# Overlapped mixing units, seeds copied into PSUM, and weight forms kept apart by size, in a hybrid RG-LRU, retention and gated-convolution block

## The chip, the cores and the metric

The kernel runs on one core of a Trainium2 chip. The time is the device time of one execution in microseconds (us), taken as the median over runs. TensorE is called PE (its weight loads PEld), VectorE DVE, ScalarE ACT, and SyncE, which issues the loads of the weights, SP.

## What is computed

One layer over 512 tokens and 16 meta tokens (528 positions), width 1024, in float32:

```python
xn = rms_norm(h, norm_mix_g[l])
z = xn @ w_in[l]
u_rnn, u_gate, q, k, v, g_ret, ga, gb = jnp.split(z, IN_SPLITS, axis=-1)
xr = causal_dwconv(u_rnn, rnn_conv_w[l], rnn_conv_b[l])
hr = rg_lru(xr, rg_a_w[l], rg_a_b[l], rg_x_w[l], rg_x_b[l], lru_lambda[l])
o_a = hr * jax.nn.gelu(u_gate)
...
o = retention(q, k, v.reshape(bsz, t, RET_HEADS, RET_DV))
o_b = head_rms(o).reshape(bsz, t, RET_HEADS * RET_DV) * jax.nn.silu(g_ret)
mixed = (jax.nn.sigmoid(ga) * (o_a @ w_branch_rnn[l])
         + jax.nn.sigmoid(gb) * (o_b @ w_branch_ret[l]))
h = h + mixed @ w_out[l]
xn = rms_norm(h, norm_ffn_g[l])
up = causal_dwconv(xn @ w_up[l], ffn_conv_w[l], ffn_conv_b[l])
gate, val = jnp.split(up, 2, axis=-1)
h = h + (jax.nn.gelu(gate) * val) @ w_down[l]
```

The end is one more RMS norm, over the 512 tokens. The change touches the values `v`, the gates `g_ret`, `ga` and `gb`, and the two branches that `mixed` sums up.

## The kernel before

**Split matmuls.** Each float32 operand is split into two float16 parts, high and low (`split`, lines 94 to 97: ACT writes the high part, L95, DVE the low one, L96), and a product takes three matmuls, high by high, high by low and low by high.

**Units of weights.** The weights are cut into units of up to 1 MB. A unit is loaded into one of three buffers `raw` (`wraw`, on SP's queue, L107), and preparation steps split it into tiles `wt` of 4 KB a partition (`wsp`, ten of them). The load of a unit takes the buffer of the unit three before it, so it waits until the last form of that one has been cut by DVE. `tick` runs preparation steps ahead of their use as long as the units from the current one on need no more than `ahead[0]` tiles; a fast unit counts four, another two.

**Fast units.** A fast unit replaces the eight block products of a 2 x 2 block multiplication by seven, with sums of weight blocks (`fast_steps`: B11, B21 with B22, three sums on DVE at L263 to L265, then T1 with T3 and T4 with T2) and sums of input blocks prepared earlier (F3, F5, F6, F7). `fast_products` (product at L929) runs them in this order, which the calls of `advance` name P1, P7, P6, P2, P5, P3, P4: B11 into a PSUM bank `pa`, T3 into `pe`, T2 onto `pa`, B21 into `pb`, T1 onto `pa`, B22 onto `pa`, T4 onto `pe`. Between them ACT copies what stands in `pa` to SBUF (`keep`, L935, tiles `kept` and `last`), and DVE adds these copies to `pb` (L954) and `pe` (L959, L967). A product has 12 matmuls in a gate unit and 24 in a unit of the second branch. At the end a function is applied: a sigmoid or another gate on ACT (L976), or a multiplication by the gate on DVE (L1244). PSUM has four banks for this from the values of head 1 on (`psum_layout(acc=2, bank=4)`), beside two `acc` tiles of two banks each.

**The stages around the change.** Values of heads 1, 2 and 3 (`fast_values`, product at L1027), each followed by the retention output and its gate (`retention_out`, `gated`), up to about 425 us; then the mix stage to 638 us. There `gate_a` runs a unit of `ga` and the first branch (`branch`, ten blocks of w_branch_rnn, tile `pm`, matmuls at L435), whose result is multiplied by the gate in `mix_first` (DVE, `m`, L1265); `head_norm(3)` sums the squares of the last head (matmul L1110, square root on ACT L1112); and `gate_b` runs a unit of `gb` and then `mix_products`, two units of w_branch_ret at once, whose result is added to `m` (L1250) and split into `mx`. The units of the two branches are mixed in the order that the lists `u_ga`, `u_ba`, `u_gb` and `u_bb` are filled in. After 638 us come the output projection, the up projection (to about 934 us) and the down projection.

**Order on an engine.** Each engine takes its instructions in the order of the program, moved by a scheduler: what stands under `tc.high_priority()` goes ahead of other ready work, and `issue_after(last_keep[0])` holds an instruction behind the last copy out of a bank (`behind_copy`, used for the late steps of a fast unit while `gating` holds). A waiting instruction holds up everything behind it on its engine.

Of the kernel before, what the change touches and what calls it, by code (L numbers as in the profile page):

```python
# [15 lines left out]
P = 128  # L16
# [38 lines left out]
def hybrid_block_kernel(ctx, tc, x, meta, norm_mix_g, w_in, conv_w, conv_b, rg_a_w, rg_a_b,  # L55
# [4 lines left out]
    xp = ctx.enter_context(tc.tile_pool(name="xp", bufs=4))  # L60
    pieces = ctx.enter_context(tc.tile_pool(name="pieces", bufs=46))
    wraw = ctx.enter_context(tc.tile_pool(name="wraw", bufs=3))
    wsp = ctx.enter_context(tc.tile_pool(name="wsp", bufs=10))
    work = ctx.enter_context(tc.tile_pool(name="work", bufs=8))
    small = ctx.enter_context(tc.tile_pool(name="small", bufs=4))
    psum = {}
# [13 lines left out]
    def bank(name):  # L80
        return psum["bank"].tile([P, 512], F32, name=name, tag="bank")
# [9 lines left out]
    def wtile(name):  # L91
        return work.tile([P, T], F32, name=name, tag="w")
# [59 lines left out]
    def add_ba():  # L152
        u_ba.append(unit(10, P, [(0, 0, kmaj(w_brnn, 0, 10, P * len(u_ba), P))]))

    def add_gate(us, o):
        us.append(unit(8, 256, [(0, 0, kmaj(w_in, 0, 8, o + 256 * len(us), 256))], fast=True))

    def add_bb():
        i = len(u_bb) // 2
        for g in range(2):  # L160
            rows = w_bret[8 * P * g:8 * P * (g + 1)].rearrange("(i j p) c -> p j i c", i=4, j=2)
            u_bb.append(unit(8, 256, [(4 * j, 0, rows[:, j, :, 256 * i:256 * i + 256]) for j in range(2)], fast=True))

    for i in range(2):
# [1 line left out]
        add_ba()  # L166
        add_gate(u_gr[3], o_gr + 1536)
        add_ba()
    add_gate(u_ga, o_ga)
    add_ba()  # L170
    add_ba()
    for i in range(4):
        add_gate(u_gb, o_gb)
        add_bb()
        if i == 0:
            add_gate(u_ga, o_ga)
        if i < 2:
            add_ba()
    u_out = [unit(2, 1024, [(0, 0, kmaj(w_out, 2 * a, 2, 0, 1024))]) for a in range(4)]
    u_up = []  # L180
    for j in range(12):
# [62 lines left out]
    def fast_steps(rv, bk, bc):  # L244


        tiles = []
        top, low = slice(0, bk), slice(bk, 2 * bk)
        left, right = slice(0, bc), slice(bc, 2 * bc)

        def cut(rows, cols):
            def run():
                t = wsp.tile([P, 2, 1024], F16, name="wt")
                src = rv[:, rows, cols]
                n = bk * src.shape[2]
                tv = [t[:, a, :n].rearrange("p (k c) -> p k c", k=bk) for a in range(2)]
                tiles.append(tv)
                split(tv[0], tv[1], src, SW)
            return run

        def sums():
            pair = rv[:, top].rearrange("p k (h c) -> p h k c", h=2)
            nc.vector.tensor_tensor(pair, pair, rv[:, :, right].rearrange("p (h k) c -> p h k c", h=2), op=ALU.add)  # L263
            nc.vector.tensor_tensor(rv[:, low, right], rv[:, top, left], rv[:, low, right], op=ALU.add)
            nc.vector.tensor_tensor(rv[:, low, left], rv[:, low, left], rv[:, low, right], op=ALU.add)  # L265

        at = {"B11": (0, 0), "B21": (1, 0), "B22": (1, bc), "T1": (2, 0), "T3": (2, bc), "T4": (3, 0), "T2": (3, bc)}

        def form(nm, a, k):
            i, c0 = at[nm]  # L270
            return tiles[i][a][:, k, c0:c0 + bc]

        def late(run):
            def behind():
                with behind_copy():
                    run()
            behind.late = True
            return behind

        wviews.append(form)  # L280
        return [cut(top, left), cut(low, slice(0, 2 * bc)), sums,
                late(cut(top, slice(0, 2 * bc))), late(cut(low, slice(0, 2 * bc)))]
# [11 lines left out]
    current = [0]  # L294

    def unit_tiles(u):
        return 4 if units[u][3] else 2

    def emit_step():
        u, run = steps[done[0]]  # L300
        while len(loaded) < min(u + 3, len(units)):
            queue(unit_load())
        run()
        done[0] += 1

    def queue(new):
# [552 lines left out]
    def rest(run):  # L859
        for _ in run:  # L860
            pass
# [58 lines left out]
    def fast_products(ws, src, func, finish, n=257):  # L920


        last_k = 4 * len(ws) - 1
        c1 = n - 257

        def product(ps, wf, xf_, first=False):
            for k in range(last_k + 1):
                for aw, ax in SPLIT:
                    nc.tensor.matmul(ps[:, :n], ws[k // 4](wf, aw, k % 4), src(xf_, ax, k),  # L929
                                     start=first and k == 0 and (aw, ax) == (0, 0), stop=k == last_k and aw == 1,  # L930
                                     skip_group_check=True)

        def keep(dst, ps, c0):
            with tc.high_priority():
                last_keep[0] = nc.scalar.activation(dst, ps[:, c0:c0 + 257], AF.Copy).ins  # L935

        kept, last = wtile("kept"), wtile("last")
        g0, g1 = wtile("g0"), wtile("g1")
        h0, h1 = slice(0, 257), slice(257, TQ)
        pa = bank("pa")  # L940
        product(pa, "B11", "A11", True)
        keep(kept[:, h0], pa, 0)
        close_tails()
        yield
        pe = bank("pe")
        product(pe, "T3", "F7", True)
        yield
        product(pa, "T2", "F6")
        keep(kept[:, h1], pa, c1)
        yield  # L950
        pb = bank("pb")
        product(pb, "B21", "A12", True)
        with tc.high_priority():
            nc.vector.tensor_tensor(g0[:, h0], pb[:, :257], kept[:, h0], op=ALU.add)  # L954
        yield
        product(pa, "T1", "F5")
        keep(last[:, h0], pa, c1)
        with tc.high_priority():
            nc.vector.tensor_tensor(g1[:, h1], pe[:, c1:n], last[:, h0], op=ALU.add)  # L959
        yield  # L960
        product(pa, "B22", "F3")
        func(g1[:, h0], pa[:, :257], -1.0, 0)
        func(g1[:, h1], g1[:, h1], -1.0, 257)
        finish(1, g1)
        product(pe, "T4", "A22")
        with tc.high_priority():
            nc.vector.tensor_tensor(g0[:, h1], pe[:, c1:n], kept[:, h1], op=ALU.add)  # L967

        def tail():
            func(g0[:, :TQ], g0[:, :TQ], 1.0, 0)  # L970
            finish(0, g0)

        tails.append(tail)
# [37 lines left out]
    def fast_values(h, others=()):  # L1011
# [46 lines left out]
        for n, (wf, src, k0, m) in enumerate(last):  # L1058
            for a in range(2):
                for g in range(4):  # L1060
# [3 lines left out]
                                     start=n == 0 and a == 0, stop=n in (1, 4) and a == 1,  # L1064
                                     tile_position=(0, 32 * g), skip_group_check=True)
        product(pa, "B22", "F3")
        done(0, 1, pa, -un)
        vt[4] = piece([P, 2, 512], F16, f"v{h}")
        split(vt[4][:, 0], vt[4][:, 1], pt, un)
# [115 lines left out]
    def gated(h):  # L1185

        other = retention_out(h + 1)
        for i in range(2):
            a = gate_unit(h, i)
            next(a)  # L1190
            if i == 0:
                head_norm(h)
            advance(a, "P7", "P6")
            next(other)
            scale_head(h, i)
            advance(a, "P2", "P5")
            next(other)
            for _ in a:
                pass
        for _ in other:  # L1200
            pass
# [4 lines left out]
    split_forms(1)  # L1206
    rest(scores(1))
    psum_layout(acc=2, bank=4)
    ahead[0] = 12
    fast_values(1, chain(scores(2), scores(3)))  # L1210
    ahead[0] = 9
    for _ in retention_out(0):
        pass
    gated(0)
    for h in range(2, 4):
        ahead[0] = 12
        fast_values(h)
        ahead[0] = 9
        gated(h - 1)
    gating[0] = False  # L1220

# [43 lines left out]
        nc.vector.scalar_tensor_tensor(m, ps, 1.0 / (SW * S_OA), sig.pop(c), op0=ALU.mult, op1=ALU.mult)  # L1265
        mix_a[c] = m

    def gate_a(i, run=None):
        if run is None:
            run = mix_unit(u_ga, i)  # L1270
            next(run)
        advance(run, "P7", "P6", "P2", "P5")
        ps = branch(u_ba, oa_of, NR)
        rest(run)
        tails.append(lambda: mix_first(2 * i, ps))

    gate_a(0)
    for i in range(2):
        run = gate_unit(3, i)
        next(run)  # L1280
        if i == 0:
            head_norm(3)
        advance(run, "P7", "P6")
        ps = branch(u_ba, oa_of, NR)
        mix_first(2 * i + 1, ps)
        scale_head(3, i)
        advance(run, "P2", "P5")
        after = mix_unit(u_ga, i + 1)
        next(after)
        rest(run)  # L1290
        gate_a(i + 1, after)
    last_branch = branch(u_ba, oa_of, NR)
    close_tails()
    mix_first(5, last_branch)
    flush(len(pending))

    def gate_b(i):

        ahead[0] = 10
        run = mix_unit(u_gb, i)  # L1300
        advance(run, "P1", "P7", "P6")
        ahead[0] = 12
        advance(run, "P2", "P5")
        rest(run)
        for _ in mix_products(i):
            tick(2)
        tick()
        ahead[0] = 10

    gate_b(0)  # L1310
    gate_a(3)
    gate_b(1)
    mix_first(7, branch(u_ba, oa_of, NR))
    gate_b(2)
    gate_b(3)
    close_tails()


# [519 lines left out]
```

## Time and profile before

| | |
|---|---|
| median of 3 runs | 1053.59 us (1053.53 to 1053.90) |
| the profiled execution | 1053.57 us |
| its span in the trace | 1051.8 us |
| granted PE clock, mean | 0.999 |
| DMA traffic | 111.52 MB, 106 GB/s over the span |
| chain that ended last | PE 86%, DVE 9%, ACT 3% |

The span is what the trace shows between the first and the last instruction; 1.8 us of the execution lie outside it. Busy shares are of the span. Matmuls are pipelined: a matmul's row says how long one takes from its start to its end, and the next starts before that, so in a run of matmuls the length of the run divided by their number is the rate. An idle time in brackets is what the engine stood before an instruction, with what ended it; "issue" is idle time without a wait that the trace shows.

### The profile page before, as it was taken

The numbers are of one execution on the slowest core, as the hardware profiler recorded it, in microseconds if no ns is written. First come the engines' busy times: TensorE is split into PE (matmuls) and PEld (weight loads), VectorE is DVE, ScalarE is ACT, GpSimd is POOL, SyncE is SP. The second block draws the span as 40 slices with busy tenths as digits, with TensorE's granted clock in tenths as the row PEclk, the third lists the DMA queues.
The fourth block names the chain that finished last, engine by engine and source line by source line (L and its number), as shares of the span: only waits on it lengthen the run. The fifth ranks groups of instructions, "written<-read, shape, count | busy, mean of one in ns | idle before, by whom it ended". The sixth has DMA issues, their size and how long they took to land.

```text
span 1051.8 us, 21653 instructions
## 1 busy us (share of the span) xinstructions
PE 1035.7 (98%) x9283; PEld 874.1 (83%) x9283; DVE 881.7 (84%) x1332; ACT 593.1 (56%) x949; POOL 6.9 (1%) x20
## 2 busy tenths in 40 slices
PE   9999999999999999999999999999999999999997
PEld 6888888866888888888888885588888888888884
DVE  6997899898779999988797785489989888988965
ACT  8668934334566758766554553384555555454432
POOL 2000000000000000000000000000000000000000
PEclk9999999999999999999999999999999999999999
DMA  9231353221113123334333365033432324124212
GB/s 295 95 132 60 121 174 128 82 82 41 41 41 121 53 95 106 97 90 157 106 106 120 121 208 174 24 98 98 144 121 81 122 87 153 44 70 139 94 41 80
DMA packets 109343, 111.52 MB, mean 106 GB/s; under 512 B 5706, under 2 KB 101168, under 8 KB 109248
## 3 DMA queue, kind: packets, MB, share of 16 engines
q1 hardware_dynamic: 108672, 109.74, 32.6%
q8 instruction: 72, 1.18, 0.5%
q10 hardware_dynamic: 288, 0.27, 0.1%
q0 software_dynamic: 288, 0.14, 0.1%
q14 instruction: 23, 0.19, 0.1%
HBM read 108.04 MB, written 2.10 MB: 105 GB/s over the span
## 4 chain that ended last, share of the span: by engine, by line
PE 86%; DVE 9%; ACT 3%; issue 1%; DMA 0%; ACTq 0%; DVEq 0%
PE ps L435 36%; PE pa L929 10%; PE P L1656 10%; PE pe L929 5%; PE ps L1373 4%; PE pm L435 4%; PE ps L449 3%; PE pb L929 3%; PE pa L1027 2%; DVE wt L96 2%; PE pa L1543 2%; PE ps L1095 2%; PE pe L1027 1%; ACT wt L95 1%; PE pe L1543 1%
## 5 line engine op out<-in xcount | busy, mean ns | idle before, releaser
L435 PEld LDWEIGHTS <-wt 128*128 128x128 f16 x3840 | 372.8, 97 | 52.8 <-DVE m L1265 1.5
L96 DVE SCALAR_TENSOR_TENSOR wt<-raw,wt 128x1024 f16<-128x1024 f32 (+2 forms) x290 | 314.9, 1101 | 56.3 <-ACT wt L95 54.9
L95 ACT ACTIVATE wt<-raw 128x1024 f16<-128x1024 f32 (+2 forms) x290 | 271.5, 957 | 128.8 <-PE P L1656 23.1
L929 PEld LDWEIGHTS <-wt 128*128 128x128 f16 x2016 | 195.3, 97 | 30.4 <-issue 3.8
L435 PE MATMUL ps<-x2h,wt 128*128 128x258 f16 (+1 forms) x1184 | 196.2, 273 | 0.0
L435 PE MATMUL ps<-xh,wt 128*128 128x258 f16 (+4 forms) x1056 | 177.0, 275 | 0.0
L435 PE MATMUL ps<-x2l,wt 128*128 128x256 f16 (+1 forms) x592 | 161.1, 272 | 0.0
L435 PE MATMUL ps<-xl,wt 128*128 128x256 f16 (+4 forms) x528 | 140.9, 274 | 0.0
L1656 PE MATMUL P<-wt,act 128*128 128x256 f16 x792 | 88.3, 273 | 0.0
L1656 PEld LDWEIGHTS <-act 128*128 128x128 f16 x792 | 77.5, 98 | 9.0
L929 PE MATMUL pa<-xs,wt 128*128 128x258 f16 x576 | 71.3, 273 | 0.4
L1521 DVE SCALAR_TENSOR_TENSOR cv<-ps,vt,cv 128x512 f32<-128x512 f32 x80 | 59.5, 747 | 9.1 <-ACT cv L1519 8.5
L263 DVE TENSOR_TENSOR raw<-raw 128x1024 f32<-128x1024 f32 x45 | 55.0, 1221 | 0.7
L435 PE MATMUL pm<-oa,wt 128*128 128x256 f16 (+1 forms) x480 | 54.1, 273 | 1.2 <-DVE m L1265 1.2
L929 PE MATMUL pa<-ob,wt 128*128 128x257 f16 x384 | 45.7, 274 | 0.7 <-ACT last L935 0.5
L1373 PE MATMUL ps<-wt,mx 128*128 128x512 f16 x192 | 44.3, 379 | 0.0
L1519 ACT ACTIVATE cv<-ps,vt,vt 128x512 f32<-128x512 f32 x40 | 30.5, 766 | 11.9 <-PE ps L435 11.9
L1543 PEld LDWEIGHTS <-wt 128*128 128x128 f16 x336 | 32.6, 97 | 4.4
L1373 PEld LDWEIGHTS <-mx 128*128 128x128 f16 x192 | 17.6, 98 | 18.5
L1027 PEld LDWEIGHTS <-xs 128*128 128x128 f16 x288 | 27.8, 98 | 5.5 <-issue 2.1
L449 PEld LDWEIGHTS <-wt 128*128 128x128 f16 x288 | 27.9, 97 | 5.0 <-issue 0.6
L1095 PE MATMUL ps<-sc,v 128*128 128x257 f16 (+4 forms) x384 | 31.6, 237 | 0.0
(328 smaller groups left out, 1497.0 us busy)
## 6 DMA issues: line engine op xcount, KB each, us to landing
raw<-in_w_in SPq DMA_DIRECT2D x34, 1024.0 KB, 5.0
raw<-in_w_up SPq DMA_DIRECT2D x24, 1024.0 KB, 5.3
raw<-in_w_down SPq DMA_DIRECT2D x48, 256.0 KB, 3.8
raw<-in_w_in SPq DMA_DIRECT2D x16, 512.0 KB, 4.9
raw<-in_w_branch_ret SPq DMA_DIRECT2D x16, 512.0 KB, 4.6
raw<-in_w_branch_rnn SPq DMA_DIRECT2D x8, 640.0 KB, 4.7
raw<-in_w_out SPq DMA_DIRECT2D x4, 1024.0 KB, 4.9
xin<-in_x SPq DMA_DIRECT2D x4, 512.0 KB, 5.8
```

The source lines that it names most:

```text
L95: a = nc.scalar.activation(hi, src, AF.Copy, scale=s)
L96: b = nc.vector.scalar_tensor_tensor(lo, src, s, hi, op0=ALU.mult, op1=ALU.subtract)
L263: nc.vector.tensor_tensor(pair, pair, rv[:, :, right].rearrange("p (h k) c -> p h k c", h=2), op=ALU.add)
L435: nc.tensor.matmul(half_of(ps, halves, hf), w(aw, k, col, P), src(ax, k, c0, n), start=k == 0 and (aw, ax) == (0, 0), stop=k == nk - 1 and ...
L449: mm = nc.tensor.matmul(half_of(ps, halves, hf), w(aw, k, col, P), src(ax, k, c0, n), start=k == 0 and (aw, ax) == (0, 0), stop=k == KD - ...
L929: nc.tensor.matmul(ps[:, :n], ws[k // 4](wf, aw, k % 4), src(xf_, ax, k), start=first and k == 0 and (aw, ax) == (0, 0), stop=k == last_k ...
L1027: nc.tensor.matmul(ps[:, TH * tt:TH * tt + TH], x_form(xf_, ax, 2 * a + k, tt * P, P), ws[a](wf, aw, k), start=first and (a, tt, k, ax, aw ...
L1095: nc.tensor.matmul(ps[:, hf, s0 - lo_i:257], vd, st[SCP[b][0]][:, sa, o:o + hi_i - s0], start=i == 0, stop=i == len(todo) - 1)
L1373: nc.tensor.matmul(ps[:, n], mx[k][:, a, c0:c0 + P], wo[k // 2](aw, k % 2, n * 512, 512), start=k == 0 and (a, aw) == (0, 0), stop=k == ks ...
L1521: nc.vector.scalar_tensor_tensor(vv_, taps[j], vt2[:, 48 * j + ch:48 * j + ch + 1], vv_, op0=ALU.mult, op1=ALU.add)
L1543: nc.tensor.matmul(ps[:, :258], w(wf, aw, k), x2_form(xf_, ax, k), start=first and k == 0 and (aw, ax) == (0, 0), stop=k == 3 and aw == 1, ...
L1656: nc.tensor.matmul(pd[:, 256 * tt:256 * tt + 256], t[:, ax, c0 + tt * P:c0 + tt * P + P], w(wf, aw, i), start=q % 6 == 0 and tt == 0 and i ...
```

## The change

1. *Seeds.* In `fast_products`, `pb` is taken from the start of a unit. ACT copies the first product from `pa` to `pb` in PSUM, and B21 accumulates on that copy. The DVE add of L954 goes. The function is applied to the first half of `g0` straight from `pb`, and to the second half separately. The tile `last` goes: `kept` serves twice. As `pb` is held from the start, a unit needs three of four banks.
2. *Overlap.* The mix stage is written with a helper, `followed`: it starts the next unit's first product, then ends the running unit. All units of `ga` and of the first branch come ahead of those of `gb` and the second branch, apart from the first unit of each list that meet in the middle, and the order of the units in memory follows.
3. *Half tiles.* A form of 512 columns (B11) goes into one of three tiles `wb` of 2 KB a partition (`wsb`); `wsp` has nine tiles of 4 KB in place of ten. A fast unit counts three tiles in `tick`, and `ahead[0]` is 9 nearly everywhere in place of 9 to 12.
4. *Preparation behind copies.* While gating, every preparation step is held behind the last copy, not only the late ones. `retention_out` and the gated stage tick at more places.

From the diff:

```diff
-    wsp = ctx.enter_context(tc.tile_pool(name="wsp", bufs=10))
+    wsp = ctx.enter_context(tc.tile_pool(name="wsp", bufs=9))
+    wsb = ctx.enter_context(tc.tile_pool(name="wsb", bufs=3))
...
-                t = wsp.tile([P, 2, 1024], F16, name="wt")
                 src = rv[:, rows, cols]
                 n = bk * src.shape[2]
+                t = wsb.tile([P, 2, 512], F16, name="wb") if n == 512 else wsp.tile([P, 2, 1024], F16, name="wt")
...
     def unit_tiles(u):
-        return 4 if units[u][3] else 2
+        return 3 if units[u][3] else 2
...
-        run()
+        with behind_copy():
+            run()
         done[0] += 1
...
-        pa = bank("pa")
+        pa, pb = bank("pa"), bank("pb")
         product(pa, "B11", "A11", True)
-        keep(kept[:, h0], pa, 0)
+        keep(pb[:, :n], pa[:, :n])
...
-        pb = bank("pb")
-        product(pb, "B21", "A12", True)
-        with tc.high_priority():
-            nc.vector.tensor_tensor(g0[:, h0], pb[:, :257], kept[:, h0], op=ALU.add)
+        product(pb, "B21", "A12")
+        func(g0[:, h0], pb[:, :257], 1.0, 0)
         yield
         product(pa, "T1", "F5")
-        keep(last[:, h0], pa, c1)
-        with tc.high_priority():
-            nc.vector.tensor_tensor(g1[:, h1], pe[:, c1:n], last[:, h0], op=ALU.add)
+        keep(kept[:, h0], pa[:, c1:n])
+        add(g1[:, h1], pe[:, c1:n], kept[:, h0])
...
         def tail():
-            func(g0[:, :TQ], g0[:, :TQ], 1.0, 0)
+            func(g0[:, h1], g0[:, h1], 1.0, 257)
             finish(0, g0)
...
+    def followed(run, make, *args):
+
+        after = make(*args)
+        next(after)
+        rest(run)
+        close_tails()
+        return after
...
-    def gate_b(i):
-
-        ahead[0] = 10
-        run = mix_unit(u_gb, i)
-        advance(run, "P1", "P7", "P6")
-        ahead[0] = 12
+    for i in range(4):
+        advance(run, "P7", "P6")
+        if i == 0:
+            mix_branch(7)
         advance(run, "P2", "P5")
-        rest(run)
-        for _ in mix_products(i):
+        flush(len(pending))
+        run = followed(run, mix_products, i)
+        for _ in range(4):
+            next(run)
             tick(2)
-        tick()
-        ahead[0] = 10
+        if i < 3:
+            run = followed(run, mix_unit, u_gb, i + 1)
```

How the order moves is seen on ACT where a unit of `gb` meets the units of the second branch. Lines of the kernel after stand one to four higher than those of the kernel before. In the kernel before, a gate unit (bank `pa_7529`, results `g1_7528`) ends like this on ACT; `wt_7698` is the first cut of a unit that comes later, out of its load `raw_7548`:

```order
L935 ACTIVATE last_7526<-pa_7529 128x257
L95 ACTIVATE wt_7661<-raw_7505 128x1024
L976 ACTIVATE g1_7528<-g1_7528 128x257
L976 ACTIVATE g1_7528<-pa_7529 128x257
L95 ACTIVATE wt_7698<-raw_7548 128x512
```

In the kernel after, a gate unit (bank `pa_7117`, results `g1_7116`) ends like this; `pa_7283` and `pb_7284` are the banks of the unit that follows it, `wb_7550` and `wb_7608` the first cuts of the two units of w_branch_ret after that, out of `raw_7262` and `raw_7363`:

```order
L936 ACTIVATE kept_7114<-pa_7117 128x257
L96 ACTIVATE wt_7369<-raw_7205 128x1024
L976 ACTIVATE g1_7116<-g1_7116 128x257
L96 ACTIVATE wb_7550<-raw_7262 128x512
L936 ACTIVATE pb_7284<-pa_7283 128x257
L96 ACTIVATE wb_7608<-raw_7363 128x512
L976 ACTIVATE g1_7116<-pa_7117 128x257
```

The function that reads `pa_7117` and so frees it has moved behind the copy and the first cuts of later units. The product that takes this bank next, `pe_7338`, waits for it. The same order stands once more, one unit on, and once one unit earlier.

The buffer of `raw_7363` is that of `raw_7020`, whose last form is `wt_7277`. On DVE, in the kernel after, from the multiplication that frees the bank `pa_6940` of the running unit to that form:

```order
L1247 SCALAR_TENSOR_TENSOR g1_6939<-pa_6940,g1_6731 128x257
L97 SCALAR_TENSOR_TENSOR wt_7259<-raw_6919,wt_7259 128x1024
L1253 TENSOR_TENSOR m_5822<-m_5822,g1_6939 128x514
L97 SCALAR_TENSOR_TENSOR wt_7268<-raw_7020,wt_7268 128x1024
L940 TENSOR_TENSOR g0_6938<-pe_6995,kept_6937 128x257
L97 SCALAR_TENSOR_TENSOR mx_7159<-m_5822,mx_7159 128x514
L1247 SCALAR_TENSOR_TENSOR g0_6938<-g0_6938,g0_6730 128x257
L264 TENSOR_TENSOR raw_7020<-raw_7020 128x4x128
L1253 TENSOR_TENSOR m_5696<-m_5696,g0_6938 128x514
L265 TENSOR_TENSOR raw_7020<-raw_7020 128x4x128
L97 SCALAR_TENSOR_TENSOR wt_7274<-raw_7020,wt_7274 128x1024
L97 SCALAR_TENSOR_TENSOR mx_7189<-m_5696,mx_7189 128x514
```

The last form, `wt_7277`, is the next row.

On ACT, after the sum of squares of head 3 (`ps_5698`), the kernel after has:

```order
L96 ACTIVATE wt_5844<-raw_5509 128x1024
L976 ACTIVATE g1_5473<-pa_5474 128x257
L96 ACTIVATE wt_5867<-raw_5509 128x1024
L96 ACTIVATE wb_5985<-raw_5750 128x512
L96 ACTIVATE wt_5939<-raw_5645 128x640
L1115 ACT_TABLE_LOAD
L1115 ACTIVATE rt_5701<-ps_5698,eps_t_85 128x514
```

The square root `rt_5701` frees `ps_5698`, whose bank the second product of the first branch, `pm_5755`, takes.

More of the change, by code (lines that the diff above doesn't have):

```diff
@@ L168, in hybrid_block_kernel @@
         add_ba()
-    add_gate(u_ga, o_ga)
-    add_ba()
+    for _ in range(2):
+        add_gate(u_ga, o_ga)
+        add_ba()
     add_ba()
@@ L173, in hybrid_block_kernel @@
         add_gate(u_gb, o_gb)
+        if i == 0:
+            add_ba()
         add_bb()
[L175 to L178, printed above, removed]
     u_out = [unit(2, 1024, [(0, 0, kmaj(w_out, 2 * a, 2, 0, 1024))]) for a in range(4)]
@@ L931, in product, with keep, add @@
                                      skip_group_check=True)
-        def keep(dst, ps, c0):
+        def keep(dst, ps):
             with tc.high_priority():
-                last_keep[0] = nc.scalar.activation(dst, ps[:, c0:c0 + 257], AF.Copy).ins
-        kept, last = wtile("kept"), wtile("last")
-        g0, g1 = wtile("g0"), wtile("g1")
+                last_keep[0] = nc.scalar.activation(dst, ps, AF.Copy).ins
+        def add(dst, a, b):
+            with tc.high_priority():
+                nc.vector.tensor_tensor(dst, a, b, op=ALU.add)
+        kept, g0, g1 = wtile("kept"), wtile("g0"), wtile("g1")
         h0, h1 = slice(0, 257), slice(257, TQ)
-        pa = bank("pa")
+        pa, pb = bank("pa"), bank("pb")
         product(pa, "B11", "A11", True)
-        keep(kept[:, h0], pa, 0)
+        keep(pb[:, :n], pa[:, :n])
         close_tails()
@@ L948, in fast_products @@
         product(pa, "T2", "F6")
-        keep(kept[:, h1], pa, c1)
+        keep(kept[:, h1], pa[:, c1:n])
         yield
-        pb = bank("pb")
-        product(pb, "B21", "A12", True)
-        with tc.high_priority():
-            nc.vector.tensor_tensor(g0[:, h0], pb[:, :257], kept[:, h0], op=ALU.add)
+        product(pb, "B21", "A12")
+        func(g0[:, h0], pb[:, :257], 1.0, 0)
         yield
         product(pa, "T1", "F5")
-        keep(last[:, h0], pa, c1)
-        with tc.high_priority():
-            nc.vector.tensor_tensor(g1[:, h1], pe[:, c1:n], last[:, h0], op=ALU.add)
+        keep(kept[:, h0], pa[:, c1:n])
+        add(g1[:, h1], pe[:, c1:n], kept[:, h0])
         yield
@@ L965, in fast_products @@
         product(pe, "T4", "A22")
-        with tc.high_priority():
-            nc.vector.tensor_tensor(g0[:, h1], pe[:, c1:n], kept[:, h1], op=ALU.add)
+        add(g0[:, h1], pe[:, c1:n], kept[:, h1])
         def tail():
-            func(g0[:, :TQ], g0[:, :TQ], 1.0, 0)
+            func(g0[:, h1], g0[:, h1], 1.0, 257)
             finish(0, g0)
@@ L1066, in fast_values @@
         product(pa, "B22", "F3")
+        ahead[0] = 12
+        tick()
+        ahead[0] = 9
         done(0, 1, pa, -un)
@@ L1194, in gated @@
             next(other)
+            tick()
             scale_head(h, i)
@@ L1197, in gated @@
             next(other)
+            tick()
             for _ in a:
@@ L1208, in hybrid_block_kernel @@
     psum_layout(acc=2, bank=4)
-    ahead[0] = 12
+    ahead[0] = 9
     fast_values(1, chain(scores(2), scores(3)))
-    ahead[0] = 9
+    current[0] = u_gr[0][0]
     for _ in retention_out(0):
-        pass
+        tick()
     gated(0)
     for h in range(2, 4):
-        ahead[0] = 12
         fast_values(h)
-        ahead[0] = 9
         gated(h - 1)
@@ L1266, in mix_first, with mix_branch @@
         mix_a[c] = m
[L1268 to L1271, printed above, removed]
+    def followed(run, make, *args):
[4 more added lines that the diff above has]
+        return after
+    def mix_branch(c, ps=None):
+        mix_first(c, branch(u_ba, oa_of, NR) if ps is None else ps)
+    run = mix_unit(u_ga, 0)
+    next(run)
+    for i in range(2):
         advance(run, "P7", "P6", "P2", "P5")
         ps = branch(u_ba, oa_of, NR)
-        rest(run)
[L1275 to L1280, printed above, removed]
+        run = followed(run, gate_unit, 3, i)
+        mix_branch(2 * i, ps)
         if i == 0:
@@ L1283, in hybrid_block_kernel @@
         advance(run, "P7", "P6")
-        ps = branch(u_ba, oa_of, NR)
-        mix_first(2 * i + 1, ps)
+        mix_branch(2 * i + 1)
         scale_head(3, i)
         advance(run, "P2", "P5")
[L1288 to L1295, printed above, removed]
-    def gate_b(i):
-        ahead[0] = 10
-        run = mix_unit(u_gb, i)
-        advance(run, "P1", "P7", "P6")
-        ahead[0] = 12
+        run = followed(run, mix_unit, u_ga, i + 1)
+    advance(run, "P7", "P6", "P2", "P5")
+    ps = branch(u_ba, oa_of, NR)
+    run = followed(run, mix_unit, u_ga, 3)
+    mix_branch(4, ps)
+    advance(run, "P7", "P6")
+    mix_branch(5)
+    advance(run, "P2", "P5")
+    ps = branch(u_ba, oa_of, NR)
+    run = followed(run, mix_unit, u_gb, 0)
+    mix_branch(6, ps)
+    for i in range(4):
+        advance(run, "P7", "P6")
+        if i == 0:
+            mix_branch(7)
         advance(run, "P2", "P5")
-        rest(run)
-        for _ in mix_products(i):
+        flush(len(pending))
+        run = followed(run, mix_products, i)
+        for _ in range(4):
+            next(run)
             tick(2)
-        tick()
-        ahead[0] = 10
[L1310 to L1315, printed above, removed]
+        if i < 3:
+            run = followed(run, mix_unit, u_gb, i + 1)
+    rest(run)
     close_tails()
```

## Prediction

> **What bounds the kernel now.** I read the page first, then the busy time stage by stage, then the matmul engine's waits, then single rows of the timeline where it stopped.
>
> ```profile
> PE 1035.7 (98%) x9283; PEld 874.1 (83%) x9283; DVE 881.7 (84%) x1332; ACT 593.1 (56%) x949; POOL 6.9 (1%) x20
> ```
>
> TensorE is busy for 1035.7 of 1051.8 us. The change leaves its work as it is, matmul for matmul, so at most the 16.1 us in which it is not busy, and the refills behind each stop, can go. The windows say where they lie (columns: window, length, PE, PEld, DVE, ACT busy with instructions, POOL, clock, DMA share, GB/s):
>
> ```profile
> 275.00:316.00 41.00, 40.78 (x438) 36.12 (x431) 32.92 (x56) 27.93 (x50) 0.00 (x0) 1.00 0.16 53
> 316.00:364.00 48.00, 47.08 (x477) 41.04 (x476) 46.29 (x68) 32.37 (x54) 0.00 (x0) 1.00 0.27 89
> 364.00:411.00 47.00, 45.94 (x468) 40.00 (x466) 44.58 (x67) 31.56 (x51) 0.00 (x0) 1.00 0.26 82
> 411.00:453.00 42.00, 39.84 (x358) 34.77 (x356) 41.84 (x68) 29.57 (x50) 0.00 (x0) 1.00 0.41 123
> 453.00:508.00 55.00, 55.00 (x503) 48.75 (x501) 47.35 (x69) 36.28 (x54) 0.00 (x0) 1.00 0.37 113
> 508.00:553.00 45.00, 44.70 (x402) 38.94 (x400) 36.24 (x50) 23.25 (x37) 0.00 (x0) 1.00 0.35 109
> 553.00:638.00 85.00, 84.27 (x754) 73.49 (x754) 65.95 (x87) 44.38 (x65) 0.00 (x0) 1.00 0.47 153
> 700.00:934.00 234.00, 234.00 (x2135) 207.01 (x2133) 209.07 (x308) 131.49 (x197) 0.00 (x0) 1.00 0.33 106
> ```
>
> From 700 to 934 us nothing is to be had: PE has no idle time. From 316 to 453 it misses 0.92 + 1.06 + 2.16 = 4.1 us, and VectorE (DVE) is 94 to 100% busy there, though only 80% in the window ahead (8.1 us idle from 275 to 316). The granted clock is 1.00 throughout, so idle time is all that counts. The waits of PE and of its weight loads name the stops (columns: us in total, times, longest), first from 300 to 640 us, then the weight loads from 453 on:
>
> ```profile
> PE pm L435 <- DVE m L1265: 1.2, 1, 1.2
> PE pe L929 <- DVE g L959: 1.0, 1, 1.0
> PE pa L1027 <- DVE wt L96: 0.9, 2, 0.5
> PE pa L1027 <- ACT wt L95: 0.9, 2, 0.4
> PE pa L929 <- ACT last L935: 0.5, 1, 0.5
> ```
> ```profile
> PEld L929 <- issue: 2.6, 9, 0.7
> ```
>
> Six long stops come from DVE, or from ScalarE (ACT), being behind with weight forms and with what clears a bank. The nine short ones lie in the mix stage, where a product of the same unit waits for the copy `last` taken out of its bank. Only the last of them, 0.65 us, has no other unit's work to put in:
>
> ```profile
> 375.98 2.50 PEld L1027 LDWEIGHTS <-xs 128*128 128x128 f16 x23 [0.27 <-issue]
> 402.08 0.99 PEld L929 LDWEIGHTS <-wt 128*128 128x128 f16 x10 [0.34 <-DVE wt L96]
> 508.65 15.87 PEld L929 LDWEIGHTS <-wt 128*128 128x128 f16 x144 [0.27 <-issue]
> 632.31 5.19 PEld L929 LDWEIGHTS <-wt 128*128 128x128 f16 x47 [0.65 <-issue]
> ```
>
> The third row also gives the matmul's rate: 15.87 us for 144, or 0.110 us each.
>
> **What the change takes away.**
>
> *Overlap in the mix stage.* The first product of the next unit (12 matmuls, 1.3 us, or 24, 2.6 us) now stands between the fifth and the last two products of the running one. The copy that these wait for takes 0.38 us (rows below). Eight short stops go: 2.6 - 0.65 = 1.9 us. The ninth is the end of the stage and stays.
>
> *Forms further ahead, one add fewer on DVE.* These are the costs of an operation in the mix stage, us in total and mean ns:
>
> ```profile
> L935 ACT ACTIVATE kept<-pa 128x257 f32<-128x257 f32 x22 | 8.3, 378 | 14.0 <-PE pa L929 13.8
> L976 ACT ACTIVATE g<-g 128x514 f32<-128x514 f32 x9 | 5.6, 627 | 1.9 <-DVE g L967 1.9
> L976 ACT ACTIVATE g<-g 128x257 f32<-128x257 f32 x8 | 3.3, 412 | 0.4 <-DVE g L959 0.4
> L976 ACT ACTIVATE g<-pa 128x257 f32<-128x257 f32 x8 | 3.1, 382 | 1.4 <-PE pa L929 1.4
> L95 ACT ACTIVATE wt<-raw 128x512 f16<-128x512 f32 x14 | 8.7, 624 | 8.3 <-PE pa L929 5.2 <-PE pm L435 3.0
> ```
> ```profile
> L96 DVE SCALAR_TENSOR_TENSOR wt<-raw,wt 128x1024 f16<-128x1024 f32 x52 | 63.1, 1221 | 9.4 <-ACT wt L95 9.0
> L264 DVE TENSOR_TENSOR raw<-raw 128x512 f32<-128x512 f32 x14 | 9.6, 687 | 0.2
> L954 DVE TENSOR_TENSOR g<-pb,kept 128x257 f32<-128x257 f32 x12 | 5.1, 423 | 10.8 <-PE pb L929 10.8
> L1250 DVE TENSOR_TENSOR m<-m,g 128x514 f32<-128x514 f32 x7 | 4.8, 689 | 0.0
> ```
>
> The add of L954 goes from 20 units: 20 x 0.42 = 8.5 us less on DVE, of which four units give back 4 x (2 x 0.42 - 0.69), 0.6 us, for two multiplies of 257 in place of one of 514. ACT gets the function in two halves at 16 units: 16 x (0.41 + 0.38 - 0.63), 2.6 us more. The seed copy costs what the copy `kept` cost, 0.38 us. Twenty-four matmuls, 2.6 us, lie between the first product and the one that accumulates on the seed, so the copy is hidden; without that cover it would cost 0.4 us each time. ACT is 56% busy and can bear its 2.6 us.
>
> With three fast units ahead instead of two to two and a half, the cuts and sums of the first gate and value units move into DVE's 8.1 us of idle time before 316. I expect the six long stops to lose their cause: 1.2 + 1.0 + 0.9 + 0.9 = 4.0 us. The profiled idle time leaves out the refill: a lone matmul takes 0.27 us where a streaming one takes 0.11, so each stop costs 0.16 more, 1.0 for six. The stops at 375.98 and 402.08 have the same cause and go for about 0.5. Together with the short ones: 4.0 + 1.0 + 0.5 + 1.9 = 7.4 us. This is an upper bound for what can go; the lower bound is 1.9, if DVE is as late as before.
>
> **What it brings back.**
>
> *After the sum of squares of head 3.* The second product of the first branch now takes the bank in which that sum stood, and ACT's square root, L1115, is what frees it. By the order ACT first does three cuts there, one of them behind a matmul of the running unit, then a table load. I count 0.3 us of waiting beyond the 2.6 us that PE has in hand: about 0.4 with its refill. Bounds: 0 and the 1.2 us that stop here today.
>
> *A cut ahead of a bank's release, twice.* All four banks are taken when units overlap, so the next unit's second product takes the bank of the running one's `pa`; ACT frees it by the function `g1<-pa`, L976. The half tiles let the first cut of the unit after next be queued directly ahead of that function, and this cut waits for a load. ACT takes its queue in order: the function, behind it the bank, and on PE the product, all wait for a load. Let T be the end of the first product of the gate unit. On PE there follow 144 matmuls until the product that takes the bank, so it is wanted at T + 15.8. The load takes its buffer when DVE has cut the last form of the unit before. DVE's queue up to there, from the end of the running unit's third product at T + 2.6, has three operations of 257, six of 514 or 512 and four low cuts of 1024: 3 x 0.42 + 6 x 0.69 + 4 x 1.22 = 10.3 us. Neighbours overlap: of these two the second starts 0.60 after the first, not 0.69.
>
> ```profile
> 447.13 0.69 DVE L96 SCALAR_TENSOR_TENSOR ob<-y,ob 128x514 f16<-128x514 f32 x1
> 447.73 0.69 DVE L96 SCALAR_TENSOR_TENSOR ob<-d,ob 128x514 f16<-128x514 f32 x1
> ```
>
> Twelve joints at 0.08 take off 1.0, so the buffer is free at T + 2.6 + 9.3 = T + 11.9, or T + 12.2 if the chain starts 0.3 late behind what stands ahead of it. The cut needs the first of the unit's two transfers. Here are two such firsts, from issue to landing, issued at 519.46 and at 526.42:
>
> ```profile
> raw<-in_w_branch_ret SPq DMA_DIRECT2D x1, 512.0 KB, 4.1
> raw<-in_w_branch_ret SPq DMA_DIRECT2D x1, 512.0 KB, 3.7
> ```
>
> It lands at T + 15.6 to T + 16.3. The half cut (0.62) and the function (0.38) follow: the bank is free at T + 16.5 to T + 17.3, so PE stands 0.7 to 1.5 us. I take 1.3, and 0.16 of refill: 1.5 each, 3.0 for two. In the kernel before that cut stood behind the function, and no wait of ACT for a load shows between 453 and 640.
>
> By the Trainium skill, "DMA: Bandwidth & Descriptors", section "Anatomy of one DMA", a transfer costs about 2.0 us and its bytes at 436 GB/s, so 3.2 us for 512 KB; an estimate from it lets PE stand 0.5 to 0.9 us less, and the sum would come out near 1048. The trace says 3.7 and 4.1 (the page's fit is for another issuing path), and I go by it. The Trainium skill's same page, section "Rules for kernel authors", says to issue a transfer early and to wait on it late; here the change does the reverse, as the rows above price it.
>
> **The sum.** The profiled execution took 1053.57 us, 1.8 of them outside the span; the median of the runs is 1053.59, the same. 1053.6 - 7.4 + 0.4 + 3.0 = 1049.6 us. A difference under 0.2%, 2.1 us, counts as no change.
>
> **The rivals.**
>
> A. *The loads come in time.* If DVE runs its queue faster than its rows say, or the landing takes 3 us, the two stops shrink to 0.3 and the time is 1053.6 - 7.4 + 0.4 + 0.6 = 1047.2; with no stop at all 1046.2. For it: all the terms are differences of a few tenths. Against it: DVE's chain starts at T + 2.6 whatever came before.
>
> B. *DVE stays the bound from 316 to 453.* For it: 41.84 of 42.00 us busy in the last of these windows, and the adds that go there are few, some 2 us. Against it: the 8.1 us of idle time just ahead. Then only the short stops go: 1053.6 - 1.9 + 3.0 = 1054.7, no measurable change; with half of the long stops gone, 1052.
>
> C. *Slower: the same cut ahead of a release costs three places, and more.* The first mix unit of the second branch has the same order on ACT; I count nothing there since its load is released earlier. One landing, issued at 557.53, took longer than those above:
>
> ```profile
> raw<-in_w_branch_ret SPq DMA_DIRECT2D x1, 512.0 KB, 5.6
> ```
>
> With such landings, or with DVE at the last cut 2 us later than I count (its queue is fuller, since one more unit is prepared ahead), each stop is 1.5 + 2.0 = 3.5 us, and it comes at three places: 3 x 3.5 = 10.5, so 1053.6 - 7.4 + 0.4 + 10.5 = 1057.1. It decides against the change from 2.3 us a place on (7.0 / 3).
>
> **How the numbers follow.** The forecast has a chance of 0.50, A 0.13, B 0.20, C 0.17. Faster: nearly all of the forecast and A, and of B a tenth, 0.63. Same: most of B, 0.19. Slower: C and a little of B, 0.18. The range goes from A's 1046.2 to a little above B's 1054.7, at 1055.2, and leaves out most of C. The likeliest case alone has 1047.8 to 1051.5, from its bounds of 0.7 and 1.5 us a stop, and of 0 and 1.2 after the sum of squares, with two of the long stops remaining at the upper end.
>
> **What would show it.** Right: no idle time of PE for `m` or `wt` from 316 to 430, none of the short stops from 508 to 620, and two stops of 1 to 1.5 us before `pe` with ACT's function as releaser, between 560 and 600, with ACT idle for a DMA just ahead of a half cut. Wrong: PE without a stop there (A); DVE over 96% and the stops for `m` and `g` still there (B); three or more stops over 2 us (C). Something else, a stop in the 700 to 934 window above all, where I count on nothing, would refute the count as a whole.

## The result and the profile after

The changed kernel takes 1060.12 us (median of six, 1058.71 to 1060.76), the kernel before 1053.62: a ratio of 1.006, with a 95% interval of 1.0048 to 1.0072. It is slower by 6.5 us, where 4.0 us less were forecast. The profiled execution has a span of 1058.6 us against 1051.8.

The page's busy line, and its chain of waits by engine:

```profile
PE 1035.2 (98%) x9283; PEld 874.9 (83%) x9283; DVE 872.5 (82%) x1316; ACT 591.9 (56%) x964; POOL 6.9 (1%) x20
...
PE 77%; DVE 16%; ACT 3%; DMA 2%; issue 1%; DVEq 0%; ACTq 0%
```

PE's busy time is nearly what it was, though some of its matmuls are slower, as shown below, and its idle time rose from 16.1 to 23.4 us. DVE has 9 us less work, where some 8 were counted. In the chain DVE's share went from 9 to 16%, and transfers, 0% before, stand at 2%. From 640 us to the end the two traces run alike, 6.7 to 6.8 us apart, and PE has no idle time from 700 to 941. Here are the waits of PE from 275 to 660 us (us in total, times, longest):

```profile
PE pm L436 <- ACT rt L1115: 4.2, 1, 4.2
PE pe L930 <- ACT g L976: 3.8, 3, 1.6
PE pa L930 <- ACT kept L936: 2.8, 3, 1.6
PE pa L1027 <- DVE wt L97: 0.8, 1, 0.8
PE ps L1098 <- ACT sq L1104: 0.7, 1, 0.7
```

Against the list of before: the waits for `m`, for `g` by DVE and for `wt` by ACT are gone, and one of those for `wt` by DVE is left. In their place stand waits for ACT, each for an instruction that takes something out of a PSUM bank: the square root, the function, the copies. ACT is 56% busy as before. What holds it shows in its own waits, from 400 to 640 us:

```profile
ACT wb L96 <- DMA raw<-in_w_branch_ret: 6.6, 5, 2.5
...
ACT wb L96 <- DMA raw<-in_w_in: 5.1, 3, 2.6
```

In the kernel before ACT waited for no load in that stretch; here it does eight times, for 11.7 us, every time with a half cut (`wb`).

**The longest stop.** ACT up to the square root that frees the bank of `pm_5755`:

```profile
430.14 1.06 ACT L96 ACTIVATE wt<-raw 128x1024 f16<-128x1024 f32 x1
433.76 0.63 ACT L96 ACTIVATE wb<-raw 128x512 f16<-128x512 f32 x1 [2.56 <-DMA raw<-in_w_in]
434.29 0.72 ACT L96 ACTIVATE wt<-raw 128x640 f16<-128x640 f32 x1
435.03 1.28 ACT L1115 ACT_TABLE_LOAD   x1
436.33 0.69 ACT L1115 ACTIVATE rt<-ps,eps_t 128x514 f32<-128x514 f32 x1
```

The square root and its table load could have begun at 431.2, when the full cut ended. They stood behind the half cut, whose load had been issued at 425.81, 1.5 us after another load, and took 7.9 us to land:

```profile
raw<-in_w_in SPq DMA_DIRECT2D x1, 1024.0 KB, 7.9
```

PE wanted the bank at 432.7 and got it at 437.07. The load accounts for 2.56 us of that. The rest, 1.6 us, is ACT's own time: the three cuts, the table load and the square root take 430.14 to 437.02, so 4.3 us without the wait, and PE had 2.6 in hand.

The 60 matmuls behind the stop took 8.40 us. In the experiment cut_const, below, the same 60 took 6.74 us behind a stop of 2.76 us. First the row of the kernel after, then that of cut_const:

```profile
437.07 8.40 PE L436 MATMUL pm<-oa,wt 128*128 128x256 f16 x60 [4.20 <-ACT rt L1115]
```
```profile
437.25 6.74 PE L436 MATMUL pm<-oa,wt 128*128 128x256 f16 x60 [2.76 <-ACT rt L1115]
```

The windows of the kernel after say why (clock in the third column from the right):

```profile
432.00:437.00 5.00, 0.87 (x8) 0.62 (x7) 2.71 (x5) 3.21 (x4) 0.00 (x0) 1.00 0.49 142
437.00:441.50 4.50, 4.43 (x26) 3.31 (x26) 4.50 (x10) 3.34 (x7) 0.00 (x0) 0.63 0.02 4
441.50:445.00 3.50, 3.50 (x34) 3.05 (x33) 2.68 (x7) 0.74 (x1) 0.00 (x0) 0.99 0.00 0
```

The granted clock falls to 0.63 behind the stop, so this one place costs 4.2 us of idle time, 0.16 of refill and 8.40 - 6.74 = 1.7 us of slow matmuls: 6.0 us.

**The two stops that were forecast.** ACT where the function `g1<-pa` frees the bank for `pe_7338`:

```profile
565.18 0.61 ACT L96 ACTIVATE wb<-raw 128x512 f16<-128x512 f32 x1
565.70 0.36 ACT L936 ACTIVATE pb<-pa 128x257 f32<-128x257 f32 x1
568.61 0.63 ACT L96 ACTIVATE wb<-raw 128x512 f16<-128x512 f32 x1 [2.54 <-DMA raw<-in_w_branch_ret]
569.14 0.37 ACT L976 ACTIVATE g<-pa 128x257 f32<-128x257 f32 x1
```

On DVE the chain that gives the buffer back runs from the multiplication at 555.24 to the last cut, which begins at 563.27 and ends at 564.5; the load is issued at 564.51 and lands after 4.1 us, at 568.6. T, the end of the gate unit's first product, is 551.75 by the weight loads' rows:

```profile
550.42 1.32 PEld L930 LDWEIGHTS <-wb 128*128 128x128 f16 x12
551.75 10.59 PEld L930 LDWEIGHTS <-wt 128*128 128x128 f16 x96
```

So the buffer was free at T + 12.7 (forecast 11.9 to 12.2), and the bank at T + 17.8. PE stood 1.62 us here and 1.53 at the next place, 30 us on; with the refill 3.5 us for two, where 3.0 were forecast. Where the first unit of the second branch begins, at 540, the cut waited 0.42 us for its load and PE didn't stop. But a place of the kind that the prediction doesn't list, between two gate units at 468.7, cost 0.9.

**Stops that the forecast doesn't have.** ACT ahead of a copy out of `pa`, for which PE waits 0.71 us:

```profile
619.75 1.06 ACT L96 ACTIVATE wt<-raw 128x1024 f16<-128x1024 f32 x1 [1.90 <-DVE raw L265]
620.71 0.37 ACT L936 ACTIVATE kept<-pa 128x257 f32<-128x257 f32 x1
```

Here it is a full cut, and it waits for DVE's sums, not for a load. The same stands at 417.4 (1.61 us, with a half cut between the full one and the copy) and, ahead of the square that PE waits for, at 286.4 (0.68).

### The profile page after: what moved, and what is told of

Same layout as the page of the kernel before. It is cut to its first block, busy times and chain, and to the rows that moved or that the text cites. A ratio compares the mean times of both kernels' runs of the same rounds, so it can differ in the third digit from the quotient of the medians.

```text
span 1058.6 us, 21620 instructions
## 1 busy us (share of the span) xinstructions
PE 1035.2 (98%) x9283; PEld 874.9 (83%) x9283; DVE 872.5 (82%) x1316; ACT 591.9 (56%) x964; POOL 6.9 (1%) x20
## 4 chain that ended last, share of the span: by engine, by line
PE 77%; DVE 16%; ACT 3%; DMA 2%; issue 1%; DVEq 0%; ACTq 0%
PE ps L436 36%; PE P L1659 10%; PE pa L930 5%; DVE wt L97 5%; PE ps L1376 4%; PE pm L436 4%; PE ps L450 3%; PE pe L930 3%; PE pa L1546 2%; PE pb L930 2%; PE pa L1027 2%; ACT wt L96 1%; DMA raw<-in_w_in 1%; DVE ob L97 1%; PE pe L1546 1%
## 5 line engine op out<-in xcount | busy, mean ns | idle before, releaser
L436 PEld LDWEIGHTS <-wt 128*128 128x128 f16 x3840 | 373.6, 97 | 56.6 <-issue 4.4
L97 DVE SCALAR_TENSOR_TENSOR wt<-raw,wt 128x1024 f16<-128x1024 f32 (+2 forms) x245 | 286.1, 1175 | 61.7 <-ACT wt L96 61.1
L96 ACT ACTIVATE wt<-raw 128x1024 f16<-128x1024 f32 (+2 forms) x245 | 245.2, 1018 | 124.3 <-DVE raw L265 30.7
L930 PEld LDWEIGHTS <-wt 128*128 128x128 f16 x1728 | 167.6, 97 | 30.4 <-issue 8.1
L96 ACT ACTIVATE wb<-raw 128x512 f16<-128x512 f32 x45 | 28.1, 625 | 25.4 <-DMA raw<-in_w_in 7.9
L97 DVE SCALAR_TENSOR_TENSOR wb<-raw,wb 128x512 f16<-128x512 f32 x45 | 30.8, 684 | 5.0 <-ACT wb L96 4.9
L936 ACT ACTIVATE kept<-pa 128x257 f32<-128x257 f32 x40 | 15.4, 385 | 33.9 <-PE pa L930 33.9
L930 PE MATMUL pa<-ob,wt 128*128 128x257 f16 x288 | 33.8, 274 | 0.5 <-ACT kept L936 0.5
```

The source lines that it names most:

```text
L96: a = nc.scalar.activation(hi, src, AF.Copy, scale=s)
L97: b = nc.vector.scalar_tensor_tensor(lo, src, s, hi, op0=ALU.mult, op1=ALU.subtract)
L436: nc.tensor.matmul(half_of(ps, halves, hf), w(aw, k, col, P), src(ax, k, c0, n), start=k == 0 and (aw, ax) == (0, 0), stop=k == nk - 1 and ...
```

## Experiments

Theory 1: ACT takes its queue in order; half cuts that wait for a load stand in it ahead of what frees a bank, and PE waits for the load through them. Rival: DVE and ACT are late as such, or one part of the change (holding behind copies, half tiles, seeds) makes the time by itself. All times are medians; the kernel before is at 1053.5 to 1053.7 us beside each.

**cut_const.** The wait for the load is taken out, and the operations are left:

```diff
-                split(tv[0], tv[1], src, SW)
+                split(tv[0], tv[1], ones[:, None, :].to_broadcast([P, 4, P]) if (bk, src.shape[2]) == (4, P) else src, SW)
```

> The changed kernel, but the first cut of a gate or second-branch unit (128 x 512, tile wb) reads a constant tile in place of its load; the values of that form are left out. ACT and DVE have the same operations, and the cut waits for no load. Theory 1 (ACT takes its queue in order, and half cuts that wait for a load stand ahead of what frees a PSUM bank): the stops of PE at 437 (4.4 us), 469 (0.9), 570 (1.8) and 599 (1.7) go or shrink to a tenth or two, those at 417 (1.8) and 621 (0.9) stay, and the time falls by 7 to 9 us, to 1051 to 1053. Rival (DVE and ACT are late as such, whatever the cuts wait for): at most 2 us go, 1058 to 1060.

1057.98 us (ratio to before 1.0046, interval 1.003 to 1.0061): 2 us gone, not 7 to 9, so by its time alone the run is where the rival had put it. The waits of PE:

```profile
PE pe L930 <- DVE g L940: 3.3, 3, 2.0
PE pm L436 <- ACT rt L1115: 2.8, 1, 2.8
...
PE pe L930 <- ACT g L976: 1.2, 4, 0.5
```

The waits for the function fell from 3.8 to 1.2, so there the load was the cause: what is left at 568 and 597 is 0.5 and 0.3 us, less than the 0.6 of the cut itself. The wait for the square root fell only to 2.8: the full cut ahead of it, which had hardly waited in the changed kernel, stood 1.87 us here until DVE had made its sums. Waits came up as well for adds on DVE (3.3 us) and, near 373, for forms (1.9). The scheduler had moved other instructions too, once these cuts were free of their loads, so the run shows that the load is a cause at the functions, and leaves open what the rest of the time hangs on.

**cut_behind.** The loads come as late as before, but the half cuts go behind what frees a bank:

```diff
+            i = nc.scalar.activation(dst, s, func, scale=sign / (SW * S_XN)).ins
+            if sign < 0 and c0 == 0:
+                last_free[0] = i
...
+        last_free[0] = nc.scalar.activation(rt[:, :TQ].rearrange("p (a b) -> p a b", a=2), ps[:, :, :257], AF.Sqrt,
...
-                split(tv[0], tv[1], src, SW)
+                with tc.issue_after(last_free[0]) if n == 512 and last_free[0] else nullcontext():
+                    split(tv[0], tv[1], src, SW)
```

> The changed kernel, with every half cut held behind the newest instruction on ACT that frees a bank in the way of PE (the function out of pa, and the square root of head_norm). It computes the same. Theory 1: the same four stops go, 1051 to 1054 us, perhaps less a little for forms that come later. Rival (DVE and ACT late as such): 1057 to 1061, with the waits moved to wt.

1050.78 us, 9.3 less than the changed kernel, and faster than before: ratio 0.9972, interval 0.9961 to 0.9983. PE's waits, and the one row of ACT's waits for a load of these units from 400 to 640 us:

```profile
PE pa L932 <- ACT kept L938: 2.6, 4, 0.7
PE pa L1033 <- DVE wt L97: 0.8, 1, 0.8
PE ps L1104 <- ACT sq L1110: 0.7, 1, 0.7
PE pe L932 <- ACT g L979: 0.4, 1, 0.4
```
```profile
ACT wb L96 <- DMA raw<-in_w_branch_ret: 0.9, 1, 0.9
```

The wait for the square root is gone, that for the function fell from 3.8 to 0.4, and nothing came in their place but three waits of 0.7 for copies. ACT now does no cut between the function and the square root:

```profile
428.64 1.28 ACT L1121 ACT_TABLE_LOAD   x1
429.93 0.69 ACT L1121 ACTIVATE rt<-ps,eps_t 128x514 f32<-128x514 f32 x1
```

The operations are those of the changed kernel, but for one table load that the new order saves ACT; PE takes its matmuls in the same order, but for a single one that moves behind the next twelve. So the order on ACT and DVE is worth 9.3 us, and work on DVE as such is not the bound. What stands ahead of a release is thus shown to be the cause. That it is the wait for a load is shown in part only: the scheduler moved full cuts along with the half cuts (at the square root three cuts, of which one waited for a load; at 417 a full cut that waited for DVE's sums), and the run doesn't tell these apart. Repeated, as cut_behind_5:

> cut_behind again, for a narrower interval: 1050.5 to 1051.0 us.

1050.63 us, ratio 0.9972, interval 0.9961 to 0.9982.

**rt_only.** Of cut_behind, only the place at the square root (the other assignment to `last_free` is left out).

> The changed kernel, with half cuts held behind the square root of head_norm alone, not behind the functions. Theory 1 (a cut that waits for its load stands ahead of what frees a bank, each place with its own price): the stop of 4.4 us before pm goes, those near 565 and 595 (1.8 and 1.7) stay; 1055 to 1057 us. Rival (the lateness moves on to the next place): 1058 to 1060.

1053.45 us, the time of before (ratio 0.9998, interval 0.9988 to 1.0007), 6.7 less than the changed kernel, and more than I expected: I had reckoned with the stop alone, not with the slow clock behind it. Here too all three cuts have gone behind the square root. The stop of 4.4, the 1.7 of slow matmuls and the 0.9 at 469 are gone; 0.5 less at 417 and 0.8 of new small stops near 443 and 446 go against each other. The other places stay:

```profile
PE pe L932 <- ACT g L978: 3.4, 3, 1.5
PE pa L932 <- ACT kept L938: 2.3, 3, 1.1
```

**not_behind.** Only late steps are held behind copies, as before:

```diff
-        with behind_copy():
-            run()
+        run()
```

> The changed kernel, where only the late steps of a fast unit are held behind a copy, as before, not every step. If the holding behind copies makes the new stops, the time falls to 1050 to 1055 us; theory 1 has the half cuts in the same places on ACT and expects 1058 to 1061.

1059.99 us (ratio 1.0058, interval 1.0043 to 1.0073), no change. The square root is again the longest wait, 4.4 us. So the holding isn't what makes these stops. That it costs time with full tiles is shown by seeds_overlap, below.

**full_tiles.** Ten full tiles, no half ones, four counted for a unit:

```diff
-    wsb = ctx.enter_context(tc.tile_pool(name="wsb", bufs=3))
...
-        return 3 if units[u][3] else 2
+        return 4 if units[u][3] else 2
```

> The changed kernel with the tiles of before: ten full tiles, none of half size, four tiles counted for a fast unit, and the same bound of 9 ahead, so two fast units ahead in place of three. Theory 1: the loads are no longer wanted so early, so the stops at 437, 469, 570 and 599 go (8.7 us), while the stops for weight forms between 316 and 375 may come back (up to 2.5 us): 1051 to 1055. Rival (the extra time comes from the overlap of units or the seeds): 1058 to 1062.

1062.24 us (ratio 1.0084, interval 1.0067 to 1.0101): theory 1 as I had put it expected 1051 to 1055, and it fell here. ACT waits for no load from 400 to 640 us, and PE has no stop at the square root, as theory 1 has it; but PE waits for the function more than ever, and for forms 5.6 us in all, where the kernel before had 1.8 and the changed kernel 0.8. The function, and the three longest rows for forms:

```profile
PE pe L929 <- ACT g L975: 4.4, 6, 1.2
PE pa L1026 <- DVE wt L96: 2.8, 2, 1.5
PE pa L929 <- ACT wt L95: 1.3, 2, 0.9
...
PE pa L929 <- DVE wt L96: 0.8, 2, 0.6
```

ACT ahead of the function says why:

```profile
569.85 1.57 ACT L95 ACTIVATE wt<-raw 128x1024 f16<-128x1024 f32 x2 [1.31 <-DVE raw L264]
571.33 0.37 ACT L975 ACTIVATE g<-pa 128x257 f32<-128x257 f32 x1
```

Without half tiles it is a full cut that stands there, and it waits for DVE's sums. So the theory has to be wider: any cut that waits, for a load or for the sums, ahead of what frees a bank. The late forms are a second cause, which theory 1 doesn't have.

**seeds_overlap.** Both of the last two edits: seeds and overlap are left.

> The changed kernel with full tiles as before and with only the late steps held behind copies: seeds and overlap are left of the change. From the two runs with one part undone each (+2.1 and -0.1 us against the changed kernel), if the parts add up: 1061 to 1063 us. If half tiles and holding hurt only together: 1051 to 1056.

1054.23 us (ratio 1.0006, interval 0.9997 to 1.0016). The time lies in the range for half tiles and holding that hurt only together, but the runs show another thing: each hurts by itself. To seeds and overlap, the holding alone adds 8.0 us (full_tiles, 1062.24), the half tiles alone 5.8 (not_behind, 1059.99), and both together 5.9 (1060.12). So the parts don't add up. The waits:

```profile
PE pe L928 <- ACT g L974: 3.5, 4, 1.2
PE pa L1025 <- DVE wt L96: 1.9, 2, 1.0
```

The stop at the square root isn't there in this order. PE's wait for the function is nearly that of the changed kernel; the waits for forms fell from 5.6 to 1.9 us. So the holding, with full tiles, makes forms late; seeds and overlap by themselves leave the time as it was before.

**before_seeds.** The kernel before with the new `fast_products` alone:

```diff
...
-        pb = bank("pb")
-        product(pb, "B21", "A12", True)
-        with tc.high_priority():
-            nc.vector.tensor_tensor(g0[:, h0], pb[:, :257], kept[:, h0], op=ALU.add)
+        product(pb, "B21", "A12")
+        func(g0[:, h0], pb[:, :257], 1.0, 0)
...
```

> The kernel before with the seeds alone: ACT copies the first product into pb, no add on DVE, the function in halves. Units overlap no more than before. If 8 us less work on DVE are what its long stops need: 1049 to 1052 us. If the order on ACT and not the work on DVE sets these stops: within 2 us of 1053.7, in either direction.

1054.59 us (ratio 1.001, interval 1.0001 to 1.0019), a little slower, as the second expectation has it. Less work on DVE halves the stop for `m` and leaves the others, and copies wait in a new place:

```profile
PE pa L929 <- ACT kept L935: 1.8, 3, 1.1
PE pe L929 <- DVE g L939: 1.2, 1, 1.2
PE pa L1026 <- DVE wt L96: 0.9, 2, 0.5
PE pa L1026 <- ACT wt L95: 0.9, 2, 0.4
PE pm L435 <- DVE m L1264: 0.6, 1, 0.6
```

The four stops for forms between 316 and 375 are as they were to within 0.01 us, so they don't hang on the adds that DVE is spared. That they are set by when the forms are queued fits the changed kernel, where three of the four are gone; no run changes that alone.

**late_behind.** cut_behind, with all steps behind the last copy in the mix stage too:

```diff
-        return tc.issue_after(last_keep[0]) if gating[0] and last_keep[0] else nullcontext()
+        return tc.issue_after(last_keep[0]) if last_keep[0] else nullcontext()
```

> cut_behind, with every preparation step held behind the last copy in the mix stage too. Theory 1 in its wider form (any form on ACT that waits for DVE's sums ahead of a copy out of a bank stops PE): the three stops of 0.9 us at 554, 583 and 611 of cut_behind go, 1047.5 to 1050 us. Rival (forms that are cut later are wanted before they are there): 1051 to 1056, with waits of PE on wt.

1054.91 us (ratio 1.0013, interval 1.0004 to 1.0022). The three stops for copies go, but each unit of the second branch gets five short waits of the weight loads for forms instead (0.2 to 0.6 us), some of them for the half cut itself. Of the matmuls' own waits, these two rows are the longest in the mix stage:

```profile
PE pe L932 <- ACT g L979: 1.1, 2, 0.8
PE pa L932 <- ACT wb L96: 1.0, 3, 0.3
```

**late_only.** The same for the late cuts alone:

```diff
-                with behind_copy():
+                with tc.issue_after(last_keep[0]) if last_keep[0] else nullcontext():
```

> cut_behind, with the late cuts of a fast unit (T1 with T3, T4 with T2) held behind the last copy in the mix stage too, and the other steps left free: a milder form of late_behind. Wider theory (what stands ahead of the copies on ACT is a late cut that waits for DVE's sums): the three stops of 0.9 us at 554, 583 and 611 go and, since the first cuts are not held, nothing comes for them: 1048 to 1050 us. If holding the late cuts alone already makes forms late, as in late_behind: 1052 to 1055.

1051.8 us (ratio 0.9983, interval 0.9974 to 0.9992), between the two expectations: the stops for copies went, but waits for forms came, 2.3 us in all:

```profile
PE pa L932 <- DVE wt L97: 2.3, 4, 0.6
```

So cut_behind is the best version found. Of its last three stops of 0.9 us, these two runs show both sides: cuts ahead of the copies delay the copies, and cuts behind them came too late.

## Why the prediction was wrong

*What goes.* Right but for one stop. The eight short stops of the mix stage are gone, and so are five of the six long ones; a stop of 1.0 us for a form stays at 370. Of the 7.4 us some 6.4 went, and 1.0 us ahead of 264 us that I hadn't counted, by the start of the same matmul in the two traces.

*After the sum of squares.* This is the step that failed: "I count 0.3 us of waiting beyond the 2.6 us that PE has in hand". I had seen the half cut ahead of the square root, but not priced its load there as I did at the other two places: I took it to be in time. The buffer was free only at 425.8, the load took 7.9 us, and the cut waited 2.56 us for it. The other part of the term was too small as well: the cuts, the table load and the root take 4.3 us without that wait, 1.7 more than the 2.6 in hand, not 0.3. And "idle time is all that counts" failed behind a stop of this length: the slow clock cost 1.7 us more. In all 6.0 us in place of 0.4. rt_only, where these cuts go behind the root, gives these 6.0 us back, by the start of the same matmuls in the two traces. My upper bound was 1.2 us, the stop that stood there before, which bounds nothing, as it was another wait.

*A cut ahead of a bank's release, twice.* The mechanism and the chain of times were right: 3.5 us against 3.0. The place at 540, counted at nothing, cost nothing; one that I hadn't listed, at 469, cost 0.9.

*Not in the sum at all:* cuts that wait for DVE's sums ahead of copies, 1.8 at 417, 0.9 at 621 and 0.7 at 286, 3.4 us. I had checked the copies by how long PE can spare them, not by what is queued ahead of them.

Together: 5.6 at the square root, 0.9 + 0.5 at the functions, 3.4 at the copies, 1.0 for the form that stays and about 0.5 for small stops that I had counted as gone are 11.9, less the 1.0 gained ahead: 10.9. The two spans differ by 6.8 where the forecast had -4.0, so 10.8.

*The rivals.* A and B are out: the loads don't come in time, and cut_behind gains with the same work on DVE. C named the right side and the right mechanism, but put it in the wrong place: its three places, at 540, 570 and 599, cost 3.5 us in all, not 10.5, and the square root decided.

## What to carry to other kernels

An engine that both prepares data ahead and clears PSUM banks can pass the waits of the preparation, and its own time, on to the matmuls. When work is started earlier, list, for each instruction that frees a bank, what is queued ahead of it and what that waits for, and price all such places alike; then hold what stands ahead of the release behind it, rather than trust the order that a scheduler works out from modelled times. Here this order was worth 9.3 us, more than the 6.4 us of stops that the change takes away. Hold no more than that: late_behind, with every step held, lost 4.1 us of it again.

## What the runs showed of the hardware

PE's granted clock fell behind a long stop. After 4.20 us without a matmul the granted clock was 0.63 over the next 4.5 us, and 60 matmuls took 8.40 us; after 2.76 us, in cut_const, it stayed at 1.00 and they took 6.74. In not_behind, after 4.39 us, it was 0.50 over 4.5 us, and they took 9.16. The Trainium skill, "TensorE: Matmul & The Clock Gate", section "What's actually happening", puts the limit at an idle window of about 3.4 us; these three stops agree with it. I had taken idle time to be all that counts, as no stop of the kernel before, once its matmuls run, is longer than 1.2 us.

A load of 1 MB that was issued 1.5 us behind one of 640 KB took 7.9 us to land, where the median in the kernel before is 5.0.
